# Layer 0's experts in plain F32, with two and four products side by side in the array's columns

## The chip, the cores and the metric

The kernel runs on one core of a Trainium2 chip. The metric is the device time of one launch in microseconds: the median over several runs. A profile of one execution goes with it. The engines are TensorE (PE; its loading of weights is listed apart as PEld), VectorE (DVE), ScalarE (ACT), GpSimd (POOL) and the queue that issues most loads, SyncE (SP).

## The reference, cut to what matters

A two-layer backbone over 256 latent and 256 context tokens of width 1024. Layer 0 mixes with a bidirectional RWKV scan and a short convolution, layer 1 with differential and neighbourhood attention. Each layer ends in a mixture of 16 SwiGLU experts, of which every token uses two:

```python
def hier_moe(h, wg, bg, we, be, w1, w3, w2):
    ...
    out = jnp.zeros((T, D), F32)
    for e in range(N_EXPERTS):
        y = (jax.nn.silu(h @ w1[e]) * (h @ w3[e])) @ w2[e]
        out = out + combine[:, e:e + 1] * y
    return out.astype(h.dtype)
```

In layer 0 all 512 tokens go through it (D = 1024, expert width 512, all F32). `modulate` (RMS norm, scale, shift) and the projection with `od_w_in` open layer 1 behind it.

## The kernel before, in words

**Lists.** Layer 0's experts run in `all0`. A router has put the tokens of each expert on a list of at most 96 places (`cap`). Per expert, POOL gathers the 96 rows of the list from HBM into `xe` (`fetch`), and `turn_rows` transposes them on PE (`xt`, two groups of four flips) into `XE`, 128 x 8 x 96: the width 1024 lies in eight chunks k over the partitions.

**Products.** `hidden(e, u)` takes the u-th of eight 512 KB loads of w1 and w3 (u 0 to 3: w1, 4 to 7: w3), each with two chunks k of 128 x 512, and adds two products to one of the expert's two PSUM banks `h`: a stationary `XE` chunk of 96 columns, a moving weight of 512 columns, an output of 96 rows. `Silu` on ACT and a product on DVE make `gg`; four flips turn it into `gT`; and four 512 KB loads of w2 give eight products into two banks `y` (the down part).

**Splits.** For experts 0 to 14 every operand is split in two F32R parts: ACT writes the rounded part (`whi`), DVE the remainder (`wlo = w - whi`), and `products` issues three F32R products for one (X hi with w hi, X hi with w lo, X lo with w hi). This is L223, `split`. Expert 15 is computed in F32 from the loads as they are.

**Order.** PE's instructions stand in the order in which the code issues them (`mm` and `flip` with `in_line`), and ACT's and DVE's, where `put` or `split` stamp them, in a second fixed order. So an instruction that waits holds back all behind it on its engine. In `all0` an expert's turn is: silu and product, the first quarter of the next expert's `hidden`, the flips of `gT`, another quarter, the down products, then the rest of the next expert's `hidden` with the flips `xt` of the expert after it between, and small tasks (`aside`: lists of places, places' numbers).

**Loads.** `load` walks `stream`, the 192 loads of 512 KB in order of use, over a ring of slots (`slots`); a load is issued by SP when the slot's last reader is done. Before the stage 12 slots serve (`early`), then 13 more (`more`: seven `w`, four `rm`, two `x3`). `without(late)` takes most away at expert 11, since their memory is used by what follows. The last two experts, 14 and 15, are not written to HBM: they are weighted (`weighted`, L808 and L809) and added by products `sc` (`last_two`). Experts 0 to 13 are written to HBM (`yD`) and gathered back per token (`room`, eight gathers behind expert 13), then weighted and added by ACT and DVE (`fetched`, L909 to L912).

**Behind it.** `norm1_scales` (L342) prepares layer 1's scale and shift: four broadcasts from HBM and two DVE operations. The weights `od_w_in` are loaded and split, the tokens normed and flipped (`nT`), and the first products `pj` of layer 1 begin. Layer 1's own experts (L213 with `w,XT`) are not changed.

Of the kernel before, what the change touches and what calls it, by code (L numbers as in the profile page):

```python
# [21 lines left out]
P = 128  # L22
D = 1024
# [56 lines left out]

NRING = 4
# [53 lines left out]
def tile_kernel(ctx: ExitStack, tc: tile.TileContext, I, out, stage=99, dbg=None):  # L135
# [229 lines left out]
    def norm1_turn(x, khi, klo):  # L365
# [3 lines left out]
        for t in (2, 3, 0, 1):  # L369
# [4 lines left out]
            for g in range(2):  # L374
                tp = ps("nT")
# [73 lines left out]
    def moe(l, tiles, cap, ng, x1, pm, pn, hhi=None, hlo=None):  # L449
# [182 lines left out]
        def experts(pe, ysb, rest, spare=None, next_norm=None):  # L632
# [144 lines left out]
            def turn_rows(e, h):  # L777
# [3 lines left out]
                if h == 0:  # L781
                    XTe[e] = [pe.tile([P, 8, cap], F32R if e < 15 else F32, tag=f"XE{i}", name="XE", bufs=2)
                              for i in range(2 if e < 15 else 1)]
# [31 lines left out]
            def all0(rest):  # L815
# [10 lines left out]
                late = ("y", "kkn", "rT", "kT", "x3", "rm0", "rm1")  # L826
# [6 lines left out]
                more = [(pe, "w", 7, None)] * 7 + [(pe, f"rm{i}", 1, h) for i in range(2) for h in range(2)] + \  # L833
# [14 lines left out]
                stream = [(0, u) for u in range(8)]  # L848
                for e in range(15):
                    stream += [(e + 1, 0), (e + 1, 1)] + [(e, u) for u in range(8, 12)] + [(e + 1, u) for u in range(2, 8)]  # L850
                stream += [(15, u) for u in range(8, 12)]
                place = {eu: i for i, eu in enumerate(stream)}
                made, loaded, there = [0], {}, {}
# [14 lines left out]
                def ready(n):  # L868

                    while made[0] < min(n, len(stream)):  # L870
                        eu = stream[made[0]]
                        made[0] += 1
                        load(made[0])
                        if eu[0] < 15:
                            there[eu] = tuple(split_tiles())
                            split(loaded[eu], *there[eu])

                def products(acc, X, es, k, w, first, last):

                    if len(X) == 1:  # L880
                        mm(acc, X[0][:, k, es], w[0], start=first, stop=last)
                        return
                    mm(acc, X[0][:, k, es], w[0], start=first, stop=False)
                    mm(acc, X[0][:, k, es], w[1], start=False, stop=False)
                    mm(acc, X[1][:, k, es], w[0], start=False, stop=last)

                def weights(e, u):
                    ready(place[e, u] + 3)
                    return there[e, u] if e < 15 else (loaded[e, u],)

                hs = {}

                def hidden(e, u):

                    w = weights(e, u)
                    if u % 4 == 0:
                        hs[e, u // 4] = ps("h", "h")[r, :]
                    for i in range(2):
                        k = u % 4 * 2 + i
                        products(hs[e, u // 4], XTe[e], r, k, [w_[:, i] for w_ in w], k == 0, k == 7)  # L900
# [49 lines left out]
                ready(2)  # L950
# [7 lines left out]
                for u in range(2, 8):  # L958
                    hidden(0, u)
                    if u == 6:  # L960
                        side.append(ids(2, 4, put))
                        aside()
                    aside()
                aside()
                fetch(2)
                for e in range(16):
                    fetch(e + 3)
                    gg = pe.tile([P, 512], F32, tag="gg", name="gg")
                    put(act(gg[r], hs.pop((e, 0)), AF.Silu))
# [1051 lines left out]
```

## Time and profile before

| what | value |
|---|---|
| median of 3 runs | 1426.29 us (1424.4 to 1427.4) |
| profiled execution | 1424.58 us, span 1422.8 us |
| mean granted TensorE clock | 0.936 of full speed |
| busy PE / DVE / ACT / POOL | 88% / 56% / 42% / 15% |
| moved by DMA | 349.21 MB, mean 245 GB/s |
| layer 0's experts, first products to the last flips `gT` | 549.9 to 863.4 us |
| flips `gT` of expert 0 to those of expert 13 | 570.8 to 817.2 us, 13 experts in 246.4 us |
| first product of layer 1 (`pj`) | 900.0 us |

How to read it: a row of the timeline gives an instruction's start and length, then in brackets the idle time of its engine before it and what ended that idle time. Products overlap in the pipeline of PE, so the distance from one start to the next is what one costs, not its length. An F32 product leaves two records of 128x512 each (the eight `y` products of one of layer 1's experts stand as x16), an F32R product one. `128*96` is the part of the array a product uses, rows by columns. Windows give busy times with counts, the granted clock (1.00 is 2.4 GHz, 0.50 is 1.2 GHz), the DMA share and the rate.

### The profile page before, as it was taken

To read this page: it belongs to the slowest core of one execution; us is meant where nothing else is said; L and a number is where in the kernel's file an instruction comes from. 1 tells how busy PE (TensorE), PEld (TensorE's weight loads), DVE (VectorE), ACT (ScalarE), POOL (GpSimd) and SP (SyncE) were. 2 spreads that over 40 slices of the span, in tenths; PEclk is the share of its full clock that TensorE was granted. 3 is DMA by queue.
4 is the path that set the end of the run, shared out by engine and by line. 5 is a ranking of instruction groups with operands and counts; after the bars stand their busy time and mean duration, and the time that the engine had idled before them with its cause. 6 is when DMAs were issued, how large, how long until landed. Compare 5 with 4: busy or idle time off the path is not lost. (4 is left out here: it accounts for less than half of the span.)

```text
span 1422.8 us, 21924 instructions
## 1 busy us (share of the span) xinstructions
PE 1250.6 (88%) x8324; PEld 790.4 (56%) x8324; DVE 790.1 (56%) x1492; ACT 590.7 (42%) x999; POOL 208.7 (15%) x229
## 2 busy tenths in 40 slices
PE   5999868888989785999999996899998699999975
PEld 0556546656757673665666662786766544433321
DVE  1326856778656635999999976955546511110003
ACT  2753322222223323877787853435656321111102
POOL 0004521333411300210111030410000000000000
PEclk9999989999999966999999997899998799999998
DMA  9686778776783646999999794741533679999564
GB/s 341 207 255 212 182 182 222 177 181 177 193 258 124 239 148 248 374 380 382 387 363 364 252 365 143 162 134 45 187 132 107 225 269 400 399 396 395 210 228 173
DMA packets 239650, 349.21 MB, mean 245 GB/s; under 512 B 95448, under 2 KB 125432, under 8 KB 239280
## 3 DMA queue, kind: packets, MB, share of 16 engines
q1 hardware_dynamic: 226240, 304.72, 63.8%
q0 software_dynamic: 10592, 34.71, 7.4%
q10 hardware_dynamic: 2704, 8.27, 1.7%
q8 instruction: 69, 1.13, 0.3%
q14 instruction: 45, 0.37, 0.1%
HBM read 326.86 MB, written 20.79 MB: 244 GB/s over the span
## 5 line engine op out<-in xcount | busy, mean ns | idle before, releaser
L223 DVE TENSOR_TENSOR wlo<-w,whi 128x1024 fp32r<-128x1024 f32 (+1 forms) x284 | 304.1, 1084 | 119.7 <-ACT whi L223 111.9
L223 ACT ACTIVATE whi<-w 128x1024 fp32r<-128x1024 f32 (+1 forms) x284 | 259.4, 928 | 180.7 <-DMA w<-in_ev_w_in_dram 71.1
L213 PE MATMUL h<-whi,XE 128*96 128x512 f32 x480 | 167.0, 404 | 1.2 <-DVE XE L223 1.2
L213 PE MATMUL pj<-hh,whi 128*128 128x512 f32 x432 | 145.7, 418 | 0.0
L213 PE MATMUL h<-w,XT 128*64 128x512 f32 x512 | 138.5, 614 | 5.1 <-issue 5.1
L213 PEld LDWEIGHTS pj<-hh,whi 128*128 128x128 f32 x432 | 81.1, 196 | 31.2 <-issue 9.0
L213 PE MATMUL h<-wlo,XE 128*96 128x512 f32 x240 | 96.9, 404 | 0.8 <-DVE wlo L223 0.8
L213 PEld LDWEIGHTS h<-whi,XE 128*96 128x96 f32 x480 | 78.3, 163 | 29.9 <-DVE XE L223 1.9
L213 PE MATMUL pj<-hh,wlo 128*128 128x512 f32 x216 | 88.3, 411 | 3.7 <-DVE wlo L223 3.6
L213 PE MATMUL ada<-w,sT 128*32 128x512 f32 x384 | 69.9, 654 | 15.8 <-DMA w<-in_ada_w_dram 9.1
L213 PE MATMUL y<-whi,gT 128*96 128x512 f32 x240 | 77.8, 395 | 0.0
L213 PE MATMUL y<-w,gT 128*64 128x512 f32 (+1 forms) x272 | 73.8, 622 | 1.5 <-ACT gT L697 1.5
L213 PEld LDWEIGHTS h<-w,XT 128*64 128x64 f32 x512 | 36.4, 138 | 63.7 <-issue 57.2
L809 DVE SCALAR_TENSOR_TENSOR ylo<-y,sw,yhi 128x512 fp32r<-128x512 f32 x16 | 12.0, 751 | 100.7 <-ACT yhi L808 100.7
L688 DVE TENSOR_TENSOR gg<-gg,h 64x512 f32<-64x512 f32 x16 | 11.1, 691 | 95.0 <-ACT gg L687 95.0
L213 PEld LDWEIGHTS pj<-hh,wlo 128*128 128x128 f32 x216 | 42.0, 194 | 18.5 <-DVE wlo L223 6.7
L213 PEld LDWEIGHTS h<-wlo,XE 128*96 128x96 f32 x240 | 39.3, 164 | 20.9 <-DVE wlo L223 9.7
L213 PEld LDWEIGHTS y<-whi,gT 128*96 128x96 f32 x240 | 38.8, 162 | 16.1 <-issue 0.3
L213 PE MATMUL y<-wlo,gT 128*96 128x512 f32 x120 | 47.5, 396 | 0.0
L1993 POOL TENSOR_TENSOR x<-x,fg 128x512 f32<-128x512 f32 x2 | 2.8, 1382 | 285.1 <-ACT sq L1992 285.1
L213 PEld LDWEIGHTS y<-w,gT 128*64 128x64 f32 (+1 forms) x272 | 24.3, 143 | 33.8 <-issue 24.1
L687 ACT ACTIVATE gg<-h 64x512 f32<-64x512 f32 x16 | 9.4, 589 | 77.9 <-PE h L213 77.9
(541 smaller groups left out, 2321.6 us busy)
## 6 DMA issues: line engine op xcount, KB each, us to landing
w<-in_moe_w_dram SPq DMA_DIRECT2D x384, 512.0 KB
w<-in_ada_w_dram SPq DMA_DIRECT2D x96, 512.0 KB
w<-in_ev_w_in_dram SPq DMA_DIRECT2D x27, 512.0 KB
w<-in_od_w_in_dram SPq DMA_DIRECT2D x24, 512.0 KB
yD<-ysb POOLq DMA_DIRECT2D x14, 384.0 KB, 6.4
sD<-wad SPq DMA_DIRECT2D x16, 256.0 KB
w<-in_ev_w_out_dram SPq DMA_DIRECT2D x8, 512.0 KB
w<-in_od_w_out_dram SPq DMA_DIRECT2D x8, 512.0 KB
```

Of the source, the lines that this page charges most:

```text
L213: inst = nc.tensor.matmul(*args, **kw)
L223: for inst in (act(hi, src, AF.Copy), V.tensor_tensor(lo, src, hi.bitcast(F32), op=ALU.subtract)):
L687: act(gg[64:128], acc[0:64], AF.Silu)
L688: V.tensor_tensor(gg[64:128], gg[64:128], acc[64:128], op=ALU.mult)
L809: V.scalar_tensor_tensor(lo, y, w, hi.bitcast(F32), op0=ALU.mult, op1=ALU.subtract))
L1993: (V if h else G).tensor_tensor(xt_[:, hs], xt_[:, hs], fg[:, hs], op=ALU.mult)
```

## The change

Layer 0's experts are computed in plain F32, with no splits of weights, of `XE` or of `gT`. Instead of 96 columns at once, the list is cut in two: places 0 to 63 (`ab`) use half the array's columns, so that two products with different weights stand side by side (w3 and w1 of one chunk k; in the down part the two halves of the output's width), and places 64 to 95 (`cc`) use a quarter, so that four do (w3 and w1 of two chunks). The four give two partial sums, which `both_halves` adds: ACT copies one, DVE adds the other. Experts 14 and 15 have unpacked F32 down products, and their weight is multiplied in `middle` instead of behind them. The loads come in another order (w1 and w3 of the same chunks together), and the ring has other slots: six `w`, three each from the tiles `whi` and `wlo` that the splits no longer need, four `rm`, two `x3`. `norm1_scales` is issued two experts earlier, at 12 instead of 14. An expert's result is written to HBM by four DMAs instead of one. In the tail, the flips `nT` get other PSUM banks, and the products `sc` another sum tile.

```diff
@@ turn_rows
-                to = [X[:, 4 * h:4 * h + 4] for X in XTe[e]]
-                if e < 15:
-                    split(acc, *to)
-                else:
-                    inorder(act(to[0], acc, AF.Copy), "moe")
+                o = XTe[e][:, 4 * h:4 * h + 4]
+                inorder(V.tensor_copy(o, acc) if h else act(o, acc, AF.Copy), "moe")
@@ all0
-                late = ("y", "kkn", "rT", "kT", "x3", "rm0", "rm1")
+                late = ("y", "kkn", "rT", "kT", "x3", "rm0", "rm1", "whi", "wlo")
...
-                more = [(pe, "w", 7, None)] * 7 + [(pe, f"rm{i}", 1, h) for i in range(2) for h in range(2)] + \
+                more = [(pe, "w", NW0, None)] * NW0 + [(pW, t, 3, None) for t in ("whi", "wlo") for _ in range(3)] + [(pe, f"rm{i}", 1, h) for i in range(2) for h in range(2)] + \
                     [(cp, "x3", 1, h) for h in range(2)]
...
+                ups = [(0, 4), (1, 5), (2, 6), (3, 7)]
...
-                    mm(acc, X[0][:, k, es], w[0], start=first, stop=False)
-                    mm(acc, X[0][:, k, es], w[1], start=False, stop=False)
-                    mm(acc, X[1][:, k, es], w[0], start=False, stop=last)
...
+                def hidden(e, q):
+                    if q == 0:
+                        hs[e] = ps("h", "h"), ps("hc", "h")
+                    w = [weights(e, u) for u in (ups[q][1], ups[q][0])]
+                    A, C = hs[e]
                     for i in range(2):
+                        for j in range(2):
+                            mm(A[64 * j:64 * j + 64, :], XTe[e][:, 2 * q + i, ab], w[j][:, i], start=(q + i == 0),
+                               stop=(q + i == 4))
+                    for i in range(2):
+                        for j in range(2):
+                            r0 = 64 * i + 32 * j
+                            mm(C[r0:r0 + 32, :], XTe[e][:, 2 * q + i, cc], w[j][:, i], start=(q == 0), stop=(q == 3))
+
+                def both_halves(o, acc):
+                    o = o[64:128]
+                    put(act(o, acc[0:64, :], AF.Copy))
+                    put(V.tensor_tensor(o, acc[64:128, :], o, op=ALU.add))
+
+                def middle(e):
+                    A, C = hs.pop(e)
+                    gg, S = (pe.tile([P, 512], F32, tag=t, name=t) for t in ("gg", "gs"))
+                    both_halves(S, C)
+                    put(act(gg[ab], A[64:128, :], AF.Silu))
+                    put(act(gg[cc], S[96:128], AF.Silu))
+                    for rs, o in ((ab, A[0:64, :]), (cc, S[cc])):
+                        if e < 14:
+                            put(V.tensor_tensor(gg[rs], gg[rs], o, op=ALU.mult))
...
+                def down(e, gT):
+                    y = [ps("y", "y") for _ in range(2)]
+                    if e > 13:
...
+                                mm(y[h][r], gT[:, f], w[:, h], start=(f == 0), stop=(f == 3))
...
+                                mm(y[0][64 * h:64 * h + 64, :], gT[:, 2 * g + i, ab], ws[i][:, h], start=(g + i == 0),
...
+                                mm(y[1][r0:r0 + 32, :], gT[:, 2 * g + i, cc], ws[i][:, h], start=(g == 0), stop=(g == 1))
...
                     elif e == 12:
                         side.append(one_hot0(14, 2, F32, put))
+                        next_norm[0]()
...
-                    if e == 14:
-                        next_norm[0]()
```

How the order moves on TensorE, inside one middle expert. The rows begin at the flips `gT` of one expert; `h`, `hc` and `xt` belong to the experts after it, `y` to this one. Before:

```order
L218 MATMUL gT<-cst,gg 128x96 x4
L213 MATMUL h<-whi,XE 96x512
L213 MATMUL h<-wlo,XE 96x512
L213 MATMUL h<-whi,XE 96x512 x2
L213 MATMUL h<-wlo,XE 96x512
L213 MATMUL h<-whi,XE 96x512
L213 MATMUL y<-whi,gT 96x512
L213 MATMUL y<-wlo,gT 96x512
```

The changed kernel, the whole turn up to the next flips `gT`:

```order
L219 MATMUL gT<-cst,gg 128x96 x4
L214 MATMUL h<-w,XE 64x512 x4
L214 MATMUL hc<-w,XE 32x512 x4
L214 MATMUL y<-w,gT 64x512 x4
L214 MATMUL y<-w,gT 32x512 x4
L214 MATMUL y<-w,gT 64x512 x4
L214 MATMUL y<-w,gT 32x512 x4
L219 MATMUL xt<-cst,xe 128x96 x4
L214 MATMUL h<-w,XE 64x512 x4
L214 MATMUL hc<-w,XE 32x512 x4
L219 MATMUL xt<-cst,xe 128x96 x4
...
L219 MATMUL gT<-cst,gg 128x96 x4
```

Where triples of 96-row products stood, fours of 64 rows and fours of 32 rows now alternate; between the second `xt` and the next `gT` there are two more such pairs of fours, the last of them for the expert after next.

On ACT, near the end of the stage: `Silu` of expert 15 (L969 before, L901 and L902 now), the first splits of `od_w_in` (`whi<-w` of 128x512), and the weighting of what was gathered (`room`). Before:

```order
L909 ACTIVATE room<-room,wk 128x1024 x2
L969 ACTIVATE gg<-h 96x512
L983 ACTIVATE gT<-gT 128x384
L909 ACTIVATE room<-room,wk 128x1024 x2
L223 ACTIVATE whi<-w 128x512 x2
L808 ACTIVATE spare<-y,sw 96x512 x2
```

And in the changed kernel:

```order
L940 ACTIVATE room<-room,wk 128x1024 x2
L893 ACTIVATE gs<-hc 64x512
L901 ACTIVATE gg<-h 64x512
L224 ACTIVATE whi<-w 128x512 x2
L902 ACTIVATE gg<-gs 32x512
L1007 ACTIVATE gT<-gT 128x384
L940 ACTIVATE room<-room,wk 128x1024 x2
L224 ACTIVATE yhi_7637<-y 96x512 x2
```

The splits of the first two `od_w_in` loads, which stood behind expert 15's middle, now stand inside it, ahead of the `Silu` of its last 32 places.

On DVE at the same place, L342 before (L343 in the changed kernel) is the scale of `norm1_scales`, and L910 to L912 (now L941 to L943) the sums of `fetched`. Before:

```order
L912 TENSOR_TENSOR x_4758<-room,x_4758 128x1024
L342 SCALAR_TENSOR_TENSOR whi<-whi,xn 128x1024 x2
L970 TENSOR_TENSOR gg<-gg,h 96x512
L910 SCALAR_TENSOR_TENSOR room<-room,wk 128x1024
L911 TENSOR_TENSOR room<-room,g2t 128x1024
```

And in the changed kernel:

```order
L942 TENSOR_TENSOR room<-room,g2t 128x1024
L224 TENSOR_TENSOR wlo<-w,whi 128x512
L943 TENSOR_TENSOR x_4758<-room,x_4758 128x1024
L894 TENSOR_TENSOR gs<-hc,gs 64x512
L907 SCALAR_TENSOR_TENSOR gg<-gg,sw,h 64x512
L224 TENSOR_TENSOR wlo<-w,whi 128x512
L907 SCALAR_TENSOR_TENSOR gg<-gg,sw,gs 32x512
```

The two scale operations have left the place ahead of expert 15's middle (they stand two experts earlier), and two remainders of `od_w_in` have come in among its steps.

## Rows read from the trace of the kernel before

**Rows 1.** Stretches of the MoE stage and behind it; one was cut separately

```profile
core 0: us, PE busy (x) PEld busy (x) DVE busy (x) ACT busy (x) POOL busy (x), PEclk, DMA share, GB/s
570.80:817.20 246.40, 237.55 (x1134) 161.14 (x1132) 223.97 (x258) 195.34 (x234) 29.95 (x27) 1.00 0.99 357
817.20:863.40 46.20, 39.03 (x167) 23.53 (x167) 30.45 (x29) 21.46 (x27) 11.81 (x13) 0.95 0.96 355
877.30:900.00 22.70, 13.43 (x39) 8.60 (x38) 20.84 (x41) 7.80 (x22) 0.54 (x1) 0.55 0.22 67
...
780.24:792.56 12.32, 12.32 (x62) 8.74 (x62) 10.85 (x11) 10.41 (x13) 1.78 (x2) 1.00 0.82 244
```

**Rows 2.** Groups of instructions, 570.8 to 817.2 us, layer 0's experts

```profile
line engine op names shapes xcount | busy us, mean ns | idle before us <-releasers
L223 DVE TENSOR_TENSOR wlo<-w,whi 128x1024 fp32r<-128x1024 f32 x157 | 190.0, 1222 | 19.7 <-ACT whi L223 17.2 <-DMA w<-in_moe_w_dram 1.0
L223 ACT ACTIVATE whi<-w 128x1024 fp32r<-128x1024 f32 x156 | 163.7, 1059 | 29.3 <-PE y L213 14.9 <-PE h L213 9.6 <-DMA w<-in_moe_w_dram 2.3
L213 PEld LDWEIGHTS h<-wlo,XE 128*96 128x96 f32 x208 | 33.6, 162 | 18.3 <-DVE wlo L223 8.6
L213 PEld LDWEIGHTS y<-wlo,gT 128*96 128x96 f32 x104 | 16.8, 161 | 9.3 <-DVE wlo L223 3.1
...
L213 PE MATMUL sw<-toks,Pg 128*96 128x2 bf16 x40 | 3.0, 178 | 0.0
```

**Rows 3.** TensorE in time, inside an expert and at its flips

```profile
start us, us, engine line op out<-in xcount [idle before <-releaser]
640.05 0.62 PE L213 MATMUL h<-whi,XE 128*96 128x512 f32 x2
640.51 0.39 PE L213 MATMUL h<-wlo,XE 128*96 128x512 f32 x1
647.10 0.55 PE L218 MATMUL gT<-cst,gg 96*128 96x96 f32 x4 [1.31 <-DVE gg L970]
647.43 0.45 PE L213 MATMUL h<-whi,XE 128*96 128x512 f32 x1
```

**Rows 4.** Waits of TensorE by releaser, 548 to 876 us

```profile
engine line waited for: us in total, times, longest us
PE gT L218 <- DVE gg L970: 15.1, 12, 7.2
PE h L213 <- DVE XE L223: 1.2, 1, 1.2
```

**Rows 5.** TensorE in time, layer 1's experts, 64-column F32 products

```profile
1157.13 1.08 PE L213 MATMUL h<-w,XT 128*64 128x512 f32 x4
1158.04 3.60 PE L213 MATMUL y<-w,gT 128*64 128x512 f32 x16
...
1162.24 1.08 PE L213 MATMUL h<-w,XT 128*64 128x512 f32 x4
1163.25 0.50 PE L213 MATMUL ac<-yhi,PT 64*128 64x512 f32 x2
```

**Rows 6.** TensorE in time, 32-column F32 products of adaLN

```profile
91.62 1.06 PE L213 MATMUL ada<-w,sT 128*32 128x512 f32 x8
92.62 0.73 PE L213 MATMUL pj<-hh,whi 128*128 128x512 f32 x2
```

**Rows 7.** All engines in time, middle of a layer 1 expert

```profile
1383.57 0.59 ACT L687 ACTIVATE gg<-h 64x512 f32<-64x512 f32 x1 [7.37 <-PE h L213]
1384.19 0.69 DVE L688 TENSOR_TENSOR gg<-gg,h 64x512 f32<-64x512 f32 x1 [7.21 <-ACT gg L687]
...
1384.94 0.46 PE L218 MATMUL gT<-cst,gg 64*128 64x64 f32 x4 [1.40 <-DVE gg L688]
```

**Rows 8.** All engines in time, end of the MoE stage

```profile
855.33 54.64 SPq L201 DMA_DIRECT2D w<-in_od_w_in_dram  x7
858.41 1.23 DVE L342 SCALAR_TENSOR_TENSOR whi<-whi,xn 128x1024 f32<-128x1024 f32 x1 [4.11 <-DMA whi<-adaD]
863.39 0.90 PE L218 MATMUL gT<-cst,gg 96*128 96x96 f32 x4 [7.17 <-DVE gg L970]
...
866.80 0.62 ACT L223 ACTIVATE whi<-w 128x512 fp32r<-128x512 f32 x1
...
872.24 0.63 ACT L223 ACTIVATE whi<-w 128x512 fp32r<-128x512 f32 x1 [4.83 <-DMA w<-in_od_w_in_dram]
...
900.00 0.79 PE L213 MATMUL pj<-rT,whi 128*128 128x256 f32 x2
```

More of the change, by code (lines that the diff above doesn't have):

```diff
@@ L78, in host_consts @@
     return c
+NW0 = 6
 NRING = 4
@@ L781, in turn_rows @@
                 if h == 0:
-                    XTe[e] = [pe.tile([P, 8, cap], F32R if e < 15 else F32, tag=f"XE{i}", name="XE", bufs=2)
-                              for i in range(2 if e < 15 else 1)]
+                    XTe[e] = pe.tile([P, 8, cap], F32, tag="XE", name="XE", bufs=2)
                 acc = ps("xt", ("ga", "ps")[h])
@@ L887, in weights @@
                 def weights(e, u):
-                    ready(place[e, u] + 3)
-                    return there[e, u] if e < 15 else (loaded[e, u],)
+                    load(place[e, u] + 3)
+                    return loaded[e, u]
                 hs = {}
[L893 to L897, printed above, removed]
-                    for i in range(2):
-                        k = u % 4 * 2 + i
-                        products(hs[e, u // 4], XTe[e], r, k, [w_[:, i] for w_ in w], k == 0, k == 7)
+                ab, cc = slice(0, 64), slice(64, 96)
@@ L949, in all0 @@
                 next(others)
-                ready(2)
                 for h in range(2):
@@ L957, in all0 @@
                 turn_rows(1, 1)
[L958 to L962, printed above, removed]
-                    aside()
-                aside()
+                for _ in range(5):
+                    aside()
+                hidden(0, 2)
+                side.append(ids(2, 4, put))
+                for _ in range(2):
+                    aside()
+                hidden(0, 3)
+                for _ in range(3):
+                    aside()
                 fetch(2)
@@ L967, in all0 @@
                     fetch(e + 3)
-                    gg = pe.tile([P, 512], F32, tag="gg", name="gg")
-                    put(act(gg[r], hs.pop((e, 0)), AF.Silu))
-                    put(V.tensor_tensor(gg[r], gg[r], hs.pop((e, 1)), op=ALU.mult))
+                    gg = middle(e)
                     if e < 15:
@@ L975, in all0 @@
                         flip(acc[:, f * cap:(f + 1) * cap], gg[r, f * 128:(f + 1) * 128], ident[r, 0:cap])
-                    acc = acc[:, 0:4 * cap].rearrange("p (f c) -> p f c", f=4)
-                    gT = [pe.tile([P, 4, cap], F32R if e < 15 else F32, tag=f"gT{i}", name="gT", bufs=2)
-                          for i in range(2 if e < 15 else 1)]
+                    gT = pe.tile([P, 4, cap], F32, tag="gT", name="gT", bufs=2)
+                    put(act(gT, acc[:, 0:4 * cap].rearrange("p (f c) -> p f c", f=4), AF.Copy))
@@ L1044, in all0 @@
                 warm(AF.Sqrt, yhi(1, 1)[r])
+                sums = pe.tile([P, 2, D], F32, tag="rm0", name="tt")
                 def last_two(a, t):
@@ L1052, in last_two @@
                         hs_ = slice(h * 512, h * 512 + 512)
-                        tt = ysb[:, a % 2, hs_]
+                        tt = sums[:, a % 2, hs_]
                         put(V.tensor_tensor(tt, acc, g2[t][:, hs_], op=ALU.mult))
@@ L1757, in spare @@
         def spare():
[L1758 to L1760 removed]
+            a = [pe.tile([P, 2, 512], F32R, name=f"yhi{i}") for i in range(2)]
+            b = pP.tile([P, 4, 512], F32R, tag="y", name="spare")
+            c = pe.tile([P, 2, 512], F32R, name="PT0")
+            return (lambda i, h: a[i][:, h]), (lambda i, h: b[:, 2 * i + h]), c.rearrange("p i (a t) -> p i a t", a=4)
         experts(pe, ysb, rest, spare, (norm1_scales, norm1_begin, norm1_end))
```

80 lines of the change are left out of this document (41 added, 39 removed).

## The prediction

> **What bounds the kernel now.** I read the windows by stage first, then the groups of instructions in the stage that changes, then the waits, then the timeline.
>
> Between the flips `gT` of expert 0 and those of expert 13 lie 246.4 us, 18.95 us for each of 13 experts [rows 1]. TensorE is busy for 237.55 of them at a granted clock of 1.00, VectorE for 223.97 and ScalarE for 195.34; the DMA share is 0.99. Four things look full, so the stage has to be taken apart.
>
> *TensorE.* An F32R product follows the one before by 0.23 us: two from 640.05 to 640.51 [rows 3]. An expert has 24 products as triples, 72 x 0.23 = 16.6 us. Its three groups of flips (one `gT`, two `xt`) take about 0.28 each (647.10 to 647.43 is 0.33 of a late one), 0.84; the small tasks' products 3.0/13 = 0.23 [rows 2]. The flips' wait for `gg` is 15.1 us in all, of which 7.2 is a single one at the end [rows 4], so 7.9/13 = 0.6. The weight loads with `wlo` sat idle until the DVE split for 8.6 + 3.1 us [rows 2], up to 0.9 an expert. The sum is 19.2 with all of the last, 18.3 with none. So the bound is TensorE, held up by about 1.3 us an expert of lateness of ScalarE and VectorE, whose work is nearly all splits: 190.0 and 163.7 us of them [rows 2].
>
> *DMA.* It is not the bound: in 780.24 to 792.56 its share falls to 0.82 and 244 GB/s [rows 1], with the products going on at TensorE's pace (busy 12.32 of 12.32). It had caught up and waited for slots.
>
> **The change part by part.**
>
> *Products.* No row has a packed product in this stage, but layer 1 has pairs of 64 columns: x4 records, one pair, in 0.91 us from 1157.13 to the next product of the same form at 1158.04, with its first pass some 0.05 longer; the x16 behind them (8 products, 4 pairs) take 3.60 from first start to last end. Less the length of a last pass, 0.59, that is 3.01 over 7 steps, 0.43 for a pass of two and 0.86 for a pair [rows 5]. Fours of 32 columns: x8 records take 1.06, less 0.59 is 0.47 for the one step, so about 0.43 + 0.43 for four products, with some 0.02 to 0.04 more on the first [rows 6]. An expert has 16 `h` products of 64 columns (8 pairs), 16 of 32 (4 fours), 8 and 8 of `y` (4 pairs, 2 fours): 18 x 0.858 = 15.44 us. That is 1.1 us less than the 16.6 of the triples.
>
> *Changes of form.* From 1162.24 the pair gives way to an `ac` product of another form after 1.01 us, against 0.91 where the same form follows [rows 5]: 0.10 for leaving a form. Entering costs the longer first pass, 0.05 (64 columns) or 0.02 (32). In the new order one turn has 15 changes: nine between 64 and 32 columns, six at the flips. 15 x 0.10 + 6 x 0.05 + 6 x 0.02 = 1.9 us. No row shows a change from 64 to 32 columns, both over all 128 rows. Bounds: nothing for these nine (then 0.8 for the other six), or a whole empty pipeline, 0.59 - 0.43 = 0.16 each [rows 5], plus entry, 2.8 for all 15. I take 1.9, since the nearest row, whose form differs in rows too, shows 0.10. The Trainium skill (TensorEngine Tiling (Array Packing), section Tiling Modes) says that changing the tiling mode, and not just the tile, drains TensorE; [rows 5] agree in kind, with 0.10 us. By that rule the nine changes cost what the six do, which is the sum I use; no run here shows a change between its 64- and 32-column modes.
>
> *Middle.* What was two steps is now six on two engines. By the durations of [rows 7] (ACT 0.59, DVE 0.69, hand-overs of 0.03 to 0.06), after the last four: copy 0.59, sum 0.69, silu of `S` 0.59, its product 0.69 with four hand-overs, about 2.75 us until the flips can start (the other silu and product lie beside). TensorE meanwhile has the next expert's first quarter, two pairs and a four, 3 x 0.86 + 0.3 for changes = 2.9 us. So it is just covered. One thing is not: the bank of the next `hc` is the bank of the last `h` (three banks, two per expert), free only after that expert's first product on DVE, some 2.0 us behind the last four, when the two pairs (1.9) are done. I take 0.2 an expert, between 0 and the whole uncovered tail, 1.5 (a chain that starts late or that other ACT and DVE work delays).
>
> *Splits, XE, gT.* The splits go, 14 us of DVE and 12 of ACT an expert, and with them the wait for `wlo` and for `gg` behind queued splits: 1.3 us an expert at most, already within the 18.95. `XE` and `gT` become one copy instead of two steps.
>
> *Sum for an expert:* 15.44 + 1.9 + 0.84 + 0.23 + 0.2 = 18.6 us against 18.95, -0.3. Over 13 experts -4.3 us. With the ends of the two unknowns: 17.3 to 20.8 each.
>
> *Loads.* Behind TensorE's 18.6 the DMA must not become late. It moves 12 loads and the rest, 246.4 x 357/13 = 6.8 MB an expert, which at the 357 GB/s of the full stage is 18.95 us, so it stands close. But in the stage its rate has gaps of waiting for slots [rows 1], and the new ring has 30 slots instead of 25, of which 18 need no split to come free. I cost it at nothing; the five more slots of lead are worth 5 x 0.52 MB / 357 GB/s = 7 us, more than the 4.3 that the stage runs ahead. The extra three writes of `yD` lie on POOL, busy 29.95 of 246.4; at 29.95/27 = 1.1 us for each operation 3.3 us an expert, covered everywhere but at expert 13, where the gathers of `room` stand behind.
>
> *Start.* The wait for the second part of `XE`, 1.2 us [rows 4], mostly goes: -1.
>
> *End (expert 13's flips to expert 15's down).* Gains: the flips of expert 15 wait 7.17 us for VectorE [rows 8], which stood in the scale operation until its broadcast came (4.11 us idle there, and a second one behind it); both stand two experts earlier now, so up to 7 us goes. Losses: expert 14's down products unpacked, 8 x 0.86 = 6.9 for 24 x 0.23 = 5.5; later writes of `yD` (1 to 3 us) ahead of the gathers that DVE's `room` sums need; and the splits of `od_w_in`, which now stand inside expert 15's middle on both engines. Before, the first such load was issued at 855.33 and split at 866.80, the second split waited for its landing until 872.24 [rows 8]. Now the slots come free some 3 to 6 us ahead of the last quarter of expert 15's products; with a landing after 4 (issue to landing of the second) to 11 us (of the first) the Silu stands until 0 to 6 us behind where it could be. Together I take -1, between -6 and +6.
>
> *Tail.* From 877.30 to 900.00 VectorE is busy for 20.84 of 22.70 [rows 1], with norm, splits of tokens, and the sums behind `sc`; TensorE begins `pj` at 900.00 [rows 8]. In the new order tokens' flips and splits stand ahead of the last `sc` sums on VectorE, so `pj` can begin some 4 sums and 4 adds of 0.69 us earlier (5.5 us), but the same work still follows and the second half of the tokens is needed soon after. I take -4, between -8 and 0.
>
> *Total.* -4.3 - 1 - 1 - 4 = -10.3. From the profiled execution's 1424.58: 1414.3. The median of the runs stands 1.7 above that execution, so 1416 for a median.
>
> **The rivals.**
>
> *A. The nine changes between 64 and 32 columns cost nothing.* For it: they keep all 128 rows and only cut columns. Against it: the measured changes. 9 x 0.10 and the entries of both forms (0.3) come to 1.1 us an expert, 14 us more: 1402. The DMA would stand nearer then (17.5 an expert against 18.95 at its full-stage rate, with 30 slots of lead, 41 us, for 13 x 1.4 = 18), but still not bind.
>
> *B. Slower: the middle is not covered.* Place: the flips `gT` and the first four `hc` of the next expert. Price: if the chain of 2.75 us starts behind a copy of `ysb`, `XE` or a list's operation, or if the third bank frees a pass later, 1.4 us more than my 0.2 stands on TensorE each time, for 13 experts 18 us: 1434. It decides from 10.3/13 = 0.8 us more an expert; wherever a `gT` row waits over 0.8 us for `gg`, it is at work. For it: the cover is 2.9 against 2.75. Against it: ScalarE and VectorE lose most of their other work. The Trainium skill (same page, section PSUM Bottleneck) warns that after packing the copies out of PSUM may become the bound; no run here shows that yet.
>
> *C. The end eats it.* The `od_w_in` loads land late, the Silu of expert 15 waits: +6 instead of -1 at the end, and the tail, bound by VectorE's same sum of work, gives 0 instead of -4: 1416 + 7 + 4 = 1427, no change.
>
> **How the numbers follow.** My forecast 0.53 (1416, with a range of its own of 1409 to 1424), A 0.15, B 0.17, C 0.15. About 0.2% (2.9 us) is what a measurement of this kernel can tell from no change. Faster: A, nearly all of the forecast (0.48) : 0.63. Same: C's larger part and a little of the forecast, 0.15. Slower: B, and what of C and the forecast lies above, 0.22. The range of 8 in 10 goes from A's 1402 to short of B's 1434: 1402 to 1433.
>
> **What would show it.** Right: distances of some 18.6 us between flips `gT`, at a clock of 1.00; inside an expert starts of pairs and fours 0.86 us apart and about 0.1 more wherever 64 gives way to 32; `gT` waits under 0.3; no DMA wait of `h` and `y`. A: starts 0.86 apart across the forms, 17.5 us. B: idle time of `gT` by `gg` or of `hc` by DVE over 0.8 us in most experts. C: ScalarE idle before the `whi` split inside expert 15's middle. The forecast is wrong altogether if the packed products run slower than those of layer 1, if the DMA waits show on TensorE, or if the granted clock falls inside the stage.

## The result, and the profile after

The changed kernel takes 1442.47 us in the median of 4 runs (1439.77 to 1445.7), the kernel before 1426.85 (1424.4 to 1429.57, 4 runs): a ratio of 1.011, with a 95% interval of 1.0082 to 1.0138. It is slower, by some 15 us, and the forecast was 1416, faster. The time lies above the range as well (1402 to 1433). The profiled execution has a span of 1441.1 us.

Where the time went shows best in stretches between points that both programs have: the first flips `xt`, the flips `gT` of experts 0, 13 and 15, the first `pj` of layer 1, the first `gT` of layer 1's experts, the end. All are starts in TensorE's timeline; the figures are us.

| stretch | before | after | difference |
|---|---|---|---|
| start to first `xt` (TensorE's instructions unchanged) | 548.3 | 553.0 | +4.7 |
| to `gT` of expert 0 | 22.4 | 21.6 | -0.8 |
| to `gT` of expert 13 | 246.4 | 245.4 | -1.0 |
| to `gT` of expert 15 | 46.2 | 50.0 | +3.8 |
| to the first `pj` | 36.6 | 31.0 | -5.6 |
| to layer 1's first `gT` | 256.7 | 274.2 | +17.5 |
| to the end | 266.1 | 266.0 | -0.1 |

So the experts are worth almost nothing, and most of the loss is behind them, in layer 1's projections, whose products were not changed. The 4.7 us ahead of the experts stay open (e7 and e8). Windows of the profile after, from `gT` of expert 0 on (columns as in [rows 1]):

```profile
core 0: us, PE busy (x) PEld busy (x) DVE busy (x) ACT busy (x) POOL busy (x), PEclk, DMA share, GB/s
574.60:820.00 245.40, 244.79 (x1449) 66.55 (x1445) 57.22 (x116) 51.65 (x91) 41.14 (x69) 1.00 0.98 352
820.00:869.90 49.90, 39.66 (x206) 13.18 (x206) 15.72 (x19) 12.09 (x19) 9.91 (x12) 0.94 0.91 334
869.90:900.90 31.00, 24.28 (x64) 13.19 (x63) 24.80 (x38) 11.82 (x23) 2.62 (x4) 0.67 0.03 7
900.90:914.60 13.70, 11.01 (x73) 10.73 (x74) 8.64 (x20) 6.07 (x16) 4.60 (x7) 0.86 0.83 173
914.60:928.40 13.80, 10.44 (x46) 8.75 (x45) 12.74 (x23) 3.82 (x8) 3.45 (x1) 0.51 0.36 115
```

The first row answers to the first of [rows 1]. VectorE is busy for 57.22 us instead of 223.97 and ScalarE for 51.65 instead of 195.34: the splits are gone. TensorE is busy for 244.79 of 245.40: it has stopped waiting, and yet needs the same time. The last two rows are the beginning of the projections: TensorE is busy for 11.01 of 13.70 and 10.44 of 13.80 us, and the granted clock in the last is 0.51. The kernel before had next to no idle TensorE there:

```profile
900.00:914.00 14.00, 13.89 (x99) 13.25 (x99) 12.33 (x28) 7.93 (x19) 6.34 (x10) 0.88 0.73 153
914.00:928.00 14.00, 14.00 (x113) 13.59 (x112) 13.36 (x17) 6.03 (x15) 9.79 (x9) 1.00 0.88 204
```

Over the whole stretch from the first `pj` to layer 1's first `gT`, before and then after:

```profile
900.00:1156.70 256.70, 239.56 (x1218) 173.87 (x1217) 141.02 (x311) 120.43 (x261) 26.55 (x27) 0.93 0.48 150
900.90:1175.10 274.20, 247.19 (x1217) 179.01 (x1217) 142.73 (x321) 121.93 (x266) 24.01 (x25) 0.91 0.47 146
```

TensorE's idle time there grows from 17.1 to 27.0 us, which is 9.9 of the 17.5. For the other 7.6 it is busy longer with the same products, at a granted clock of 0.91 instead of 0.93.

**The experts.** TensorE's timeline of one turn, which answers to [rows 3]:

```profile
650.07 0.55 PE L219 MATMUL gT<-cst,gg 96*128 96x96 f32 x4
650.56 1.94 PE L214 MATMUL h<-w,XE 128*64 128x512 f32 x8
652.42 1.07 PE L214 MATMUL hc<-w,XE 128*32 128x512 f32 x8
653.42 5.80 PE L214 MATMUL y<-w,gT 128*64 128x512 f32 x32
659.15 0.55 PE L219 MATMUL xt<-cst,xe 96*128 96x96 f32 x4
659.62 1.94 PE L214 MATMUL h<-w,XE 128*64 128x512 f32 x8
```

Two pairs of `h` products (x8) take 1.86 us from their start to that of `hc`, where 0.86 for each pair would be 1.72; `hc` to `y` takes 1.00 instead of 0.86; the down part, x32, takes 5.73 instead of 12 x 0.43 = 5.15; a group of flips takes 0.48. The turn from one `gT` to the next is 18.7 us. The only wait of `gT` for `gg` in all 13 experts is this one:

```profile
engine line waited for: us in total, times, longest us
PE gT L219 <- DVE gg L905: 0.4, 1, 0.4
```

**The end of the stage.** All engines in time, at expert 15's middle:

```profile
857.15 1.07 PE L214 MATMUL hc<-w,XE 128*32 128x512 f32 x8
...
858.93 0.59 ACT L901 ACTIVATE gg<-h 64x512 f32<-64x512 f32 x1
864.49 0.63 ACT L224 ACTIVATE whi<-w 128x512 fp32r<-128x512 f32 x1 [4.97 <-DMA w<-in_od_w_in_dram]
865.15 0.69 DVE L224 TENSOR_TENSOR wlo<-w,whi 128x512 fp32r<-128x512 f32 x1 [5.16 <-ACT whi L224]
...
867.01 0.69 DVE L894 TENSOR_TENSOR gs<-hc,gs 64x512 f32<-64x512 f32 x1
...
869.91 0.90 PE L219 MATMUL gT<-cst,gg 96*128 96x96 f32 x4
...
871.39 10.05 PE L214 MATMUL y<-w,gT 128*96 128x512 f32 x16 [0.58 <-ACT gT L1007]
```

The last `hc` products start at 857.15 and are through at 858.2. ScalarE copies one partial sum, does its first silu and then stands 4.97 us until a load of `od_w_in` lands, VectorE as long behind it; the sum `gs` comes at 867.01 and the flips at 869.91. TensorE stands idle in the meantime, and the eight down products that follow need 10.05 us, partly at half clock, where 8 x 0.86 = 6.9 would do. Before, these flips came at 863.39 [rows 8].

**The projections.** All engines in time:

```profile
906.84 0.69 DVE L1084 TENSOR_TENSOR x<-tt,x 128x512 f32<-128x512 f32 x1
...
907.61 0.34 ACTq L1838 DMA_DIRECT2D c<-in_cst_dram  x1
...
913.50 1.10 PE L214 MATMUL rp<-xw,c 128*128 128x256 f32 x4 [2.69 <-DMA c<-in_cst_dram]
913.53 4.52 POOL L1902 TENSOR_TENSOR xn<-xn,c 128x2048 f32<-128x2048 f32 x1 [4.76 <-DMA c<-in_cst_dram]
...
914.55 4.12 DVE L1878 TENSOR_TENSOR xw<-xw,c 128x256 f32<-128x256 f32 x2
...
919.72 0.69 PE L219 MATMUL nT<-cst,xn 128*128 128x128 f32 x2 [2.69 <-DVE xn L364]
```

The constants `c` of layer 1's rotation are loaded at 907.61, right behind the addition to `x` at 906.84 that reads the last part of the new sum tile. `rp` waits for them until 913.50. At 913.53 GpSimd, which waited for the same load, begins its addition of the mask to the neighbourhood bias, and two operations of VectorE which take 0.42 each alone take 4.12 beside it. What stands behind them is late, the norm and the flips of tokens 0 and 1 among it (919.72), and the clock falls. In the kernel before, the same load, the addition, and a VectorE operation beside it:

```profile
877.34 0.34 ACTq L1808 DMA_DIRECT2D c<-in_cst_dram  x1
...
913.13 3.38 POOL L1870 DMA_DIRECT2D xn<-in_relb_dram  x5 [7.44 <-PE nT L218]
917.71 2.04 POOL L1870 DMA_DIRECT2D xn<-in_relb_dram  x3 [1.20 <-issue]
...
919.39 5.31 DVE L1848 TENSOR_TENSOR xw<-xw,c 128x256 f32<-128x256 f32 x1
...
919.76 4.64 POOL L1871 TENSOR_TENSOR xn<-xn,c 128x2048 f32<-128x2048 f32 x1
```

There, too, VectorE stands beside GpSimd (5.31 us), but the constants were loaded 30 us earlier and all tokens were flipped by 913, so TensorE didn't wait. GpSimd's order differs as well: before, its first addition stands behind all 16 of its loads (eight at 900.22, the last eight from 913.13 on, when the flips of tokens 0 and 1 are done); in the changed kernel it stands ahead of the second eight, which begin at 928.66.

### The profile page after: what moved, and what is told of

Its sections match the earlier page's. It is cut to its first block, busy times and chain, and to the rows that moved or that the text cites. A ratio compares the mean times of both kernels' runs of the same rounds, so it can differ in the third digit from the quotient of the medians.

```text
span 1441.1 us, 22145 instructions
## 1 busy us (share of the span) xinstructions
PE 1267.0 (88%) x8700; PEld 687.0 (48%) x8700; DVE 590.1 (41%) x1329; ACT 425.6 (30%) x835; POOL 218.1 (15%) x271
## 5 line engine op out<-in xcount | busy, mean ns | idle before, releaser
L214 PE MATMUL y<-w,gT 128*64 128x512 f32 (+2 forms) x736 | 163.0, 612 | 2.1 <-ACT gT L698 1.5
L224 DVE TENSOR_TENSOR wlo<-w,whi 128x512 fp32r<-128x512 f32 (+1 forms) x104 | 84.7, 828 | 111.5 <-ACT whi L224 107.4
L214 PE MATMUL h<-w,XE 128*64 128x512 f32 x512 | 125.4, 611 | 3.0 <-ACT XE L790 2.5
L224 ACT ACTIVATE whi<-w 128x512 fp32r<-128x512 f32 (+1 forms) x104 | 69.9, 700 | 155.4 <-DMA w<-in_ev_w_in_dram 73.0
L214 PEld LDWEIGHTS y<-w,gT 128*64 128x64 f32 (+2 forms) x736 | 44.9, 131 | 101.7 <-issue 91.4
L214 PE MATMUL hc<-w,XE 128*32 128x512 f32 x512 | 68.2, 605 | 0.1
L894 DVE TENSOR_TENSOR ysb<-y,ysb 64x512 f32<-64x512 f32 x14 | 9.7, 695 | 139.1 <-ACT ysb L893 139.1
L214 PEld LDWEIGHTS h<-w,XE 128*64 128x64 f32 x512 | 31.3, 137 | 57.1 <-issue 48.1
L1020 POOL DMA_DIRECT2D yD<-ysb x28 | 15.1, 545 | 171.7 <-ACT ysb L1016 171.7
L1316 DVE TENSOR_TENSOR pr<-T,X 128x8 f32<-128x8 f32 (+14 forms) x120 | 35.7, 298 | 4.0 <-DMA X<-xs 0.6
## 6 DMA issues: line engine op xcount, KB each, us to landing
sD<-wad SPq DMA_DIRECT2D x16, 256.0 KB
```

The lines of the kernel that those rows point to most:

```text
L214: inst = nc.tensor.matmul(*args, **kw)
L224: for inst in (act(hi, src, AF.Copy), V.tensor_tensor(lo, src, hi.bitcast(F32), op=ALU.subtract)):
L894: put(V.tensor_tensor(o, acc[64:128, :], o, op=ALU.add))
L1020: nc.gpsimd.dma_start(yD[e * cap:e * cap + 64, hs_], o[64 * h:64 * h + 64, 0:512])
L1316: V.tensor_tensor(pr[:, :, 0:t], T[:, 0:t, :].rearrange("p s j -> p j s"), X[:, 0:t, t][:, None, :].to_broadcast([P, 8, t]), op=ALU.mult)
```

## The experiments

The timed comparison scatters more in these runs than in the first: the kernel before lay between 1422.13 and 1447.14 in 30 runs. So each experiment is read from the stretches of its profile first, and from the time second. The time from the first `xt` to the end is 874.5 us in the profile of before and 888.1 after. "Idle" is TensorE's idle time in the stretch from `pj` to layer 1's `gT`, and the clock is the mean granted in it. The ratios are those recorded with the runs, not quotients of the medians beside them (for e1 that would be 1.0057).

| kernel | `gT` 0 to 13 | to `gT` 15 | to `pj` | to layer 1's `gT` | idle, clock in it | `xt` to end | median us (runs) | ratio to before |
|---|---|---|---|---|---|---|---|---|
| before | 246.4 | 46.2 | 36.6 | 256.7 | 17.1, 0.93 | 874.5 | 1428.86 (30), 1427.70 (18) | |
| after | 245.4 | 50.0 | 31.0 | 274.2 | 27.0, 0.91 | 888.1 | 1442.47 (4) | 1.011 [1.0082, 1.0138] |
| e1, splits behind | 245.4 | 45.2 | 30.2 | 271.0 | 28.7, 0.93 | 881.4 | 1436.96 (9) | 1.0039 [1.0006, 1.0073] |
| e2, constants early | 245.4 | 50.1 | 29.6 | 265.1 | 25.6, 0.94 | 879.0 | 1434.47 (10) | 1.0040 [1.0016, 1.0063] |
| e3, both | 245.4 | 46.7 | 29.7 | 265.5 | 26.1, 0.94 | 875.7 | 1430.22 (10) | 1.0018 [0.9993, 1.0042] |
| e4, old tail | 245.4 | 50.3 | 35.5 | 262.0 | 22.5, 0.94 | 881.6 | 1437.05 (10) | 1.0067 [1.0049, 1.0086] |
| e5, e3 and masks on VectorE | 245.4 | 43.6 | 30.1 | 259.0 | 21.0, 0.95 | 866.5 | 1424.34 (12) | 0.9968 [0.9940, 0.9995] |
| e6, e5 and fewer changes | 239.4 | 43.0 | 29.7 | 261.7 | 19.8, 0.93 | 862.0 | 1415.80 (7) | 0.9908 [0.9873, 0.9943] |
| e7, before again | 246.4 | 45.0 | 36.2 | 256.0 | 17.0, 0.94 | 873.0 | 1423.89 (1) | |
| e8, changed again | 245.4 | 50.1 | 29.7 | 269.9 | 27.0, 0.92 | 882.6 | 1437.99 (1) | |

**e1: the splits put behind expert 15's middle.** The hook stands between the last two `fetched`; the first projection takes the tiles from there.

```diff
+                        load(len(stream))
+                        slots[:] = base
+                        turn[0] = 0
                         for n in (2, 3):
                             fetched(n, put)
+                            if n == 2:
+                                token[0] = "moe"
+                                next_norm[3]()
+                                token[0] = None
...
+        def first_weights():
+            first["ws"] = [wload(I["od_w_in"][0][h * 512:(h + 1) * 512, 0:256], 4, 256) for h in range(2)]
...
+                split(first["ws"][h][:, :, 0:128], first["s"][0][:, 4 * h:4 * h + 4, :], first["s"][1][:, 4 * h:4 * h + 4, :])
```

> The changed kernel, with the first two od_w_in splits put behind expert 15's middle by a stamp (their loads are issued ahead, on the same base slots). In the changed kernel ScalarE stood 4.97 us and VectorE 5.16 us for these loads inside the middle; the flips gT of expert 15 came at 869.9, 11.7 us after the last hc product at 858.2. My theory: the middle alone takes 2.8 us, so the flips come some 8 us earlier against expert 13's (41 us behind instead of 49.9), and the down products behind them at full clock; end to end -8 us, 1434. Rival (the work on VectorE behind it was bound anyway, or the projections wait for the constants whatever comes before): under -3 us, 1440 or more.

The stretch to `gT` of expert 15 fell by 4.8 us, not 8, and the whole behind `xt` by 6.7. TensorE's rows show why not 8:

```profile
867.03 2.82 PE L214 MATMUL h<-w,XE 128*64 128x512 f32 x8 [2.82 <-DMA w<-in_moe_w_dram]
...
874.62 0.81 PE L219 MATMUL gT<-cst,gg 96*128 96x96 f32 x4 [0.28 <-DVE gg L907]
```

The flips now come 3.0 us behind the last `hc` product (871.6), as the chain of six steps predicts, and not 11.7. But expert 15's last weights land late in this profile, after 2.82 us of waiting, and the products behind that wait run slower (1.82 us for the last x8 of `hc`, against 1.07). The edit isn't shown to bring this wait: the changed kernel has 0.53 of it in its first profile and 2.76 in e8. So the place of the splits cost 8.7 us at the flips, of which 4.8 came back.

**e2: the constants in memory of their own.**

```diff
-        c1 = pA.tile([P, NC1], F32, name="c1")
-        nc.scalar.dma_start(c1, I["cst1"])
+        c1 = ada_pool.tile([P, 512], F32, tag="abt", name="c1")
+        c2 = cp.tile([P, 256], F32, tag="sT", name="c2")
+        nc.scalar.dma_start(c1, I["cst1"][:, 0:512])
+        nc.scalar.dma_start(c2[:, 0:192], I["cst1"][:, 512:704])
```

> The changed kernel, with layer 1's constants c1 in memory of their own (two tiles of the adaLN's that are long done) instead of memory that the experts' pool gives back; nothing else is moved. In the changed kernel this load was issued at 907.6, right behind the last addition that reads the new sum tile in that pool, against 877.3 before; the product rp waited for it until 913.5, and the stretch from the first pj to layer 1's first gT took 274.2 us against 256.7. My theory: the late constants start this (rp, then the collision of POOL's relb addition with the rotary operations on VectorE, then the half clock from 914.6 to 928.4); the stretch comes back to some 260 us, -13 us, 1429. Rival (the projections are late because tokens 0 and 1 are normed and flipped behind, or because pj now has the three h banks and PSUM is opened anew behind the first projection): c1 lands early, rp doesn't wait for it, and the stretch stays above 270; 1440.

The stretch behind `pj` fell from 274.2 to 265.1: two thirds of what I expected. The rival's mark, over 270, was not met either. All engines in time:

```profile
904.58 0.70 PE L214 MATMUL rp<-xw,c 128*128 128x256 f32 x2
...
910.22 4.92 POOL L1904 TENSOR_TENSOR xn<-xn,c 128x2048 f32<-128x2048 f32 x1 [5.15 <-DMA xn<-in_relb_dram]
...
910.71 5.58 DVE L224 TENSOR_TENSOR wlo<-w,whi 128x512 fp32r<-128x512 f32 x2
...
915.74 0.58 PE L214 MATMUL pj<-rT,wlo 128*128 128x256 f32 x1 [3.51 <-DVE wlo L224]
...
922.47 5.44 POOL L1903 DMA_DIRECT2D xn<-in_relb_dram  x8 [7.33 <-PE nT L219]
```

`rp` runs at 904.58 without a wait, 9 us earlier (6.9 counted from `pj`). But GpSimd's addition, no longer held by the constants, now begins at 910.22, 9.5 us earlier than in the kernel before. It stands ahead of GpSimd's second eight loads, as in the changed kernel, and the flips that free its own tile end 4.0 us earlier than before (896.1 against 900.1). It falls on the splits that the projection waits for: two of 0.68 take 5.58, and `pj` stands 3.51 us. So one wait took the place of the other: TensorE's idle time fell by 1.4 us only, from 27.0 to 25.6, and the rest of the 9.1 came with the granted clock (0.91 to 0.94). How much of that the constants bring is not shown, since the changed kernel itself has 269.9 in e8. End to end the ratio fell from 1.011 to 1.004, and the two intervals don't overlap.

**e3: both.** The edits of e1 and e2 together.

> Both edits of the two runs above. My theory: they add, -21 us, 1421, a little faster than before (1426.5). Rival (the gain of one is given back by the other, since VectorE's backlog at the end is the bound): 1429 to 1434. In all four runs the part ahead of the experts is the same program as before; in the profile of the changed kernel it was 4.6 us longer, with other dips of the clock. If that is scatter of one execution, it will lie between -3 and +6 in these four; if it comes with the changed program, near +4.6 in all.

They add for the most part: 888.1 to 875.7 us behind `xt`, 12.4 where 6.7 and 9.1 make 15.8 and 21 was expected (in e3 the last weights of expert 15 wait 3.30 us). By the median it is level with before, the interval includes 1. I had expected it to be faster; GpSimd's addition is left, which e5 takes up. The part ahead of `xt` was 551.4 to 561.0 in the four, never below 551.

**e4: the old tail under the new experts.** The tiles `yhi`, `ylo`, `PT` and the sums back in the pool below the experts' one, one bank for `nT`, and `psum(ps=2, pj=4, t4=2)` ahead of the first projection:

```diff
-            a = [pe.tile([P, 2, 512], F32R, name=f"yhi{i}") for i in range(2)]
-            b = pP.tile([P, 4, 512], F32R, tag="y", name="spare")
-            c = pe.tile([P, 2, 512], F32R, name="PT0")
+            a, b, c = (pP.tile([P, 4, 512], F32R, tag=t, name="spare") for t in ("y", "kkn", "rT"))
...
-                        tt = sums[:, a % 2, hs_]
+                        tt = ysb[:, a % 2, hs_]
...
-    alias.update(pj="h", t4="y")
+    psum(ps=2, pj=4, t4=2)
```

> The changed kernel with the old tail: weighted outputs, places and sums of experts 14 and 15 in the old tiles, one PSUM bank for the flips nT, PSUM opened anew ahead of the first projection; experts, ring and order as changed, the od_w_in splits still inside expert 15's middle. My theory: the constants come early again by this too (the experts' pool is done early), the flips nT come later, some 4 us after expert 15; the stretch from pj to layer 1's first gT is back at 257 to 260, total -10 us, 1432. Rival (the tail as such is no loss, the late weights of the projections are): no change, 1440.

In the sum of the two stretches less than expected: `pj` comes 4.5 us later again (35.5), the projections are 12.2 us shorter (262.0), together -7.7 against the first profile of the changed kernel, and -2.1 against e8. TensorE's idle time falls by 4.5 us in the projections (27.0 to 22.5) and grows by 4.1 ahead of `pj` (6.7 to 10.8). GpSimd's order is that of before again: its first addition stands behind all 16 loads, at 928.98. So the new tail brought the other order, and the old one gives back part of the loss in the projections; that the new tail is a loss in sum is not shown by this run alone. The rest of 5.3 against before stands with two waits of `pj` for the split of a weight, 4.5 us in all.

**e5: the masks added on VectorE, behind the third projection.** On top of e3:

```diff
-            G.tensor_tensor(Bm[qt].rearrange("p h r c -> p (h r) c"), Bm[qt].rearrange("p h r c -> p (h r) c"),
-                            c2[:, 128:192][:, None, :].to_broadcast([P, 32, 64]), op=ALU.add)
...
         proj1(512, 512, ev_dk)
+        for qt in range(2):
+            V.tensor_tensor(Bm[qt].rearrange("p h r c -> p (h r) c"), Bm[qt].rearrange("p h r c -> p (h r) c"),
+                            c2[:, 128:192][:, None, :].to_broadcast([P, 32, 64]), op=ALU.add)
```

> As e3 (splits behind, constants early), and the two additions of the mask to the neighbourhood bias moved from GpSimd to VectorE, behind the third projection. In e2 GpSimd's addition ran from 910.22 for 4.92 us, and a VectorE operation that takes 0.68 took 5.58 for two beside it; the split of a weight came late, pj waited 3.51 us for it, and the clock fell to 0.5 from 914.8 to 921.4. In the kernel before the same addition ran from 919.76, when all flips nT were done, and nothing waited. My theory: the tail of the change, by flipping tokens 2 and 3 earlier, starts this addition earlier, into the splits that the projections wait for; without it the stretch from pj to layer 1's first gT falls from 265.5 in e3 to 257 to 260, and from the first xt to the end 875.7 to about 869, 1424. Rival (it is VectorE's backlog of sums and norms, which stays): over 264, no change against e3.

259.0 in the projections, as expected, and 866.5 behind `xt`, 2.5 better than expected: at the end of the stage the last weights waited 1.1 us and not 3.30 as in e3, which this edit doesn't explain. By the median it is a little faster than the kernel before. Of the 6.5 us against e3, 5.1 are idle time of TensorE (26.1 to 21.0). So the collision was the second part of the loss in the projections. The kernel before with this edit was not run; TensorE didn't wait there beside the collision shown above. (An addition takes 2.29 us on VectorE, 4.7 on GpSimd.)

**e6: three of the fifteen changes of width taken out.** On top of e5:

```diff
+                    for part in ((narrow, wide) if q == 3 else (wide, narrow)):
+                        part()
...
+                        for part in ((narrow, wide), (wide, narrow))[g]:
+                            part()
```

> As e5, and 3 of the 15 changes of column width in an expert's turn taken out: the last quarter of hidden does its 32-column products first, so that the next quarter follows with 64 columns, and the down part goes 32, 64, 64, 32. If a change costs what the changed kernel's rows show, 0.52 from the last start to the next first instead of 0.43, and a longer first pass, 0.12 to 0.15 each, the 13 experts fall from 245.4 to 240 us; the sum of fours in the middle also starts earlier. End to end -5 against e5, 1418. Rival (the change of width hides, the 18.7 us come from something else): 245.

13 experts took 239.4 us, 6.0 less: 0.46 an expert, 0.15 for each change taken out. TensorE in time:

```profile
652.37 5.62 PE L214 MATMUL y<-w,gT 128*32 128x512 f32 x32
...
661.27 0.55 PE L219 MATMUL xt<-cst,xe 96*128 96x96 f32 x4
661.75 1.06 PE L214 MATMUL hc<-w,XE 128*32 128x512 f32 x8
662.74 3.65 PE L214 MATMUL h<-w,XE 128*64 128x512 f32 x16
```

The down part, x32, takes 5.55 us with two changes inside, where it took 5.73 with three, and the step into it from `hc`, of the same width, takes 0.88 instead of 1.00; the two quarters' `h` products, x16, stand as one row. The window of the 13 experts, columns as above:

```profile
575.50:814.90 239.40, 238.71 (x1448) 69.96 (x1444) 57.24 (x116) 51.72 (x91) 41.31 (x69) 1.00 0.99 361
```

TensorE is still busy for nearly all of it. The projections, which this edit doesn't touch, took 261.7 against 259.0 in e5, with less idle time (19.8) and a lower clock (0.93). e6 is the version that beats both: 1415.80 us, a ratio of 0.9908 [0.9873, 0.9943] to the kernel before.

**e7 and e8: both kernels once more.**

> The kernel before, one more profile, for the part ahead of the experts, which has the same program in all these kernels: the first flips xt came at 548.3 in the first profile of before, and between 551.4 and 561.0 in the five of the changed kernel and its variants. If that is scatter of the clock, this profile lies between 548 and 561 too, more likely above 550; if the changed program brings it, 548 again.

> The changed kernel, one more profile. Theory: the stretches behind the first xt repeat to within 1 us (13 experts 245.4, gT of 13 to gT of 15 50, from there to pj 31, pj to layer 1's first gT 274), since waits set them; the part ahead of the first xt does not repeat (548 to 561). Rival (the loss in the projections is a matter of where the clock happens to fall): that stretch differs by over 4 us.

`xt` came at 549.1 in the kernel before, at 553.4 in the changed one. With the others that makes 548.3 and 549.1 for before, and 551.4 to 561.0 in eight profiles of the changed experts. Ahead of `xt`, TensorE, VectorE and GpSimd have the same instructions in both programs, but not all is the same: in the changed one SyncE issues six more loads of expert weights (between 513 and 524 us in its first profile), and ScalarE has two splits fewer. These come too late to explain the difference: the product `u<-Bt,Q` that begins at 318.0 us in the first profile of before begins at 317.2 in e7, and at 322.1 to 330.4 in the other eight. Nor is it the mean clock alone: it is 0.92 ahead of `xt` in the first profile of before and in e8, which is 5.0 us later. Why the changed programs would be later there is open, and with two profiles of before against eight it may still be scatter. In the comparison of medians less of it is left: after less before is 15.6 us, of which 13.6 lie behind `xt` in the first pair of profiles.

Behind `xt`, e8 repeats the experts and the stretch to `gT` of expert 15 to 0.1 us, and the stretch to `pj` to 1.3. The projections came 4.3 us shorter (269.9), more than the 4 us that I had named as the rival's mark. TensorE's idle time in them did repeat, in both kernels: 27.0 us twice after, 17.0 and 17.1 before. Single waits didn't (the one for the constants is 4.91 us in e8 and 2.69 in the first profile). The clock differs: at 0.5 from 913.8 to 917.2 and 920.6 to 927.5 instead of 914.9 to 928.5. So waits account for 9.9 to 10.0 us of the loss; the rest goes with the clock, 7.6 us in the first pair and 3.8 in e7 and e8. My 1 us was too narrow for that stretch, and differences between single profiles there are uncertain by some 4 us.

## Why the prediction was wrong

**The step that failed is the tail.** The prediction followed it up to the first `pj` and said -4 us, between -8 and 0. That much came: the stretch to `pj` is 5.6 us shorter. It was costed as if a `pj` that begins earlier were the gain; for what stands behind it the prediction has "the same work" and no term. The new sum tile, the weighted outputs and the places (these two were moved as well, which the section on the change doesn't say) were so put at nothing. They lie in the experts' pool, whose memory layer 1's constants take over; so the constants' load waits for the last sum, 30 us later than before, and GpSimd's first addition comes ahead of its second eight loads, beside work of VectorE that TensorE waits for.

The projections became 17.5 us longer in the first pair of profiles and 13.9 in e7 and e8: 9.9 to 10.0 us more idle time of TensorE, and the rest at a lower clock. In the first profile after, TensorE had work for 10.44 of 13.80 us from 915 to 928, at 0.51. With the constants early and the addition moved (e5 against the changed kernel), 6.0 of the 9.9 us of idle time came back. What each of the two costs alone is not shown, since either wait takes the place of the other (e2), nor how much of the clock follows from the waits.

**The experts: the mechanism and the turn were right, the gain too small to carry the rest.** 18.6 us was forecast for a turn, 18.7 stands in the profile for nine of the 13; the packed products cost 0.86 a pair and a four, and a change between 64 and 32 columns costs 0.14, leaving and entering together, as [rows 5] and [rows 6] had led me to expect. The stage gives -1.0 instead of -4.3: flips and changes together cost 3.2 us a turn and I had 1.92 + 0.84 = 2.76 (the groups of flips take 0.48 with what they change, on both sides), and four of the 13 turns with small tasks between the products take 19.0 to 19.4 (mean of all 18.88). The 0.2 for the bank did not come. By the Trainium skill (TensorEngine Tiling (Array Packing), section Tiling Modes) a changed tiling mode drains TensorE; the trace agrees in so far as a change between 64 and 32 columns over the same 128 rows costs 0.14 to 0.15 us, and e6 gives 6.0 us back by three changes less. Rival A, that these changes are free, falls; so does rival B, the uncovered middle: `gT` waited once, 0.4 us.

**The end: rival C named the mechanism, and priced it too low.** The splits inside expert 15's middle were named as a loss of 0 to 6 us and averaged with gains to -1; they cost 8.7 at the flips, and the stretch came to +3.8, inside the -6 to +6 given for it. The other half of rival C, a tail that gives 0 up to `pj`, did not come. The gain set against the loss, the scale operations moved away, fits e5 and e6, which are without the loss and have 43.6 and 43.0 against 46.2; no run tests it alone.

**The start** gave -0.8 for a forecast -1.

**Two sums** of the prediction are a little off and change nothing: 9 x 0.10 + 0.3 is 1.2 us and not 1.1 (rival A), and 30 slots of lead are 30 x 0.52 MB / 357 GB/s = 44 us and not 41.

**The loads** did not bind in the 13 experts, as I said (no wait for a load in them). At expert 15 they did, for 0.53 to 3.30 us in all eight profiles of the changed experts and in neither of before, which I had not foreseen.

The sum of what was forecast was -10.3; e5, with the three losses taken out, has -8.0 behind `xt`. That the two are close is luck in part: the 13 experts gave -1.0 of the -4.3 forecast, the end -2.6 for -1, the stretch to `pj` -6.5 for -4, and the projections still cost 2.3. What was missing was the reach of the tail's edits behind the first product of the next layer.

## What to carry to other kernels

A tile that is moved into another pool moves the end of that pool's life: look up who takes over its memory, and when that one's first load used to be issued. Where GpSimd's work moves to another time, ask what VectorE does then, and keep elementwise work of GpSimd away from the splits that TensorE waits for. Packed narrow products should follow others of their width: here 15 changes a turn left 1.0 us of gain over 13 experts, and 12 changes left 7.0.

## What the runs showed of the hardware that was not expected

- GpSimd's addition over 128x2048 (4.5 to 5 us) held VectorE up nearly for its whole length in these profiles: operations of 0.42 took 4.12 for two, of 0.68 took 5.58 for two, and in the kernel before one of 0.42 took 5.31.
- Fours of 32-column products and pairs of 64-column ones cost the same pass of 0.43 us, and the change between them, at 2.4 GHz, 0.14 to 0.15 us with the longer first pass.
- TensorE was busy for 244.79 of 245.40 us in the changed stage and 237.55 of 246.40 before [rows 1]: the busy share rose by three points at the same time. A busy share says nothing of what the work is worth.
- The part ahead of the first `xt`, with the same instructions on TensorE, ended between 548.3 and 561.0 us in ten profiles, at mean granted clocks of 0.89 to 0.92; the clock alone doesn't order them.
- TensorE's idle time in the projections repeated to 0.1 us in two profiles of each kernel (17.1 and 17.0, 27.0 and 27.0), while the length of the same stretch differed by up to 4.3 us, with the granted clock.
